# Where the operands of a matmul start: new addresses for the rows of x and for the weight slots

## The chip, the cores and the metric

The kernel runs on one core of one Trainium2 chip. The metric is the time of one execution on the device, in microseconds (us).

## The reference

One layer of a hybrid encoder on 512 tokens of 2048 features, with 16 learned meta tokens ahead of them (528 rows). What matters here is where its matrix products are:

```
hn = rmsnorm(h_res, norm_in_g)
P = hn @ w_in                       # 528 x 2048 times 2048 x 8320
Pr, Pc = P[..., :4224], P[..., 4224:]
...                                 # Pr: r, k, v, gate, two low-rank inputs -> RWKV-7 state recurrence
...                                 # Pc: B, C, h, gate -> gated causal convolution of width 3
h_res = h_res + concat(y_a, y_b) @ w_out
return rmsnorm(h_res, norm_f_g)[16:]
```

All of it is in float32. The kernel keeps that precision with products in the round format float32r: each operand is split into a high part and a low part (the remainder), and a product is made of three matmuls: high by high, high by low, low by high.

## The kernel before

**Input projection.** `x`, transposed and multiplied by the norm's gain, lies in SBUF as two tiles of 16 rows of 528 numbers, `xh` (high) and `xl` (low); row `kt` holds features 128 kt to 128 kt + 127 of all 528 tokens, one feature a partition. `w_in` is cut into 65 tiles of 128 output columns. The list `plan` gives their order: the low-rank tile, then k, r, B, v and so on, for eight pairs of heads (k, r, v, g) and eight groups of the convolution (C, h, B, gc). A weight tile comes in as two transfers of 128 x 1024 numbers (`raw`, three buffers), and each half of a transfer, a quarter of the tile, is split into `hi` and `lo` of 128 x 512 (`split_w`, lines 121 to 126: the copy on ACT at line 124, the subtraction on DVE or POOL at line 125). There are six buffers for `hi` and six for `lo`; a quarter is split about six quarters before its use (`prefetch`).

`steps` (lines 305 to 317) issues the matmuls: for a quarter, each range of columns, each of four `kt`, and the three products

```
for n, (ww, xx) in enumerate(((hi, xh), (hi, xl), (lo, xh))):
    nc.tensor.matmul(ps[r], ww[:, w], xx[:, kt, a:b], ...)
```

Here `ww[:, w]`, 128 x 128, is the operand that is loaded into the array (the trace has each load as an instruction of PEld), and `xx[:, kt, a:b]` is the one that streams past it. The ranges are FULL (k, v and the low-rank tile: columns 0 to 264 and 264 to 528), TAIL (r, g, C, h: 14 to 272 and 272 to 528) and REAL (B, gc: 16 to 528 in one). A tile of two ranges has 96 matmuls, one of REAL has 48; line 314 has 5,466 matmuls in all.

**Order of the work.** TensorE's program is written by hand: `mains` is a generator that yields after each main matmul, and the other stages (low-rank products, Gram matrices, the inversion and the recurrence over chunks) call `fill` to put so many main matmuls between their own. So while weights remain, PE has work beside nearly every wait.

**Output projection.** `units` lists 56 products of 128 x 1024 weights with sums and differences of the mixed activations (a Strassen-like scheme with seven products instead of eight). Here the operands change places: the activations (`parts`, tiles m0 and m1, and `sform`, tiles S1, S3, S4, S5) are loaded into the array, and the split weights, again `hi` and `lo`, stream with 512 columns (`product`, line 1220). Their splits are made by ACT (line 1192) and DVE (line 1193) in the same six buffers, `oh` and `ol`. Only the last product's weights have buffers of their own, the `home` tiles, laid over the S tiles of the first half; they stream at line 1220 with 512 columns and at line 1422 with 256.

**Where tiles lie.** A pool hands out memory in the order in which its tiles are asked for, each rounded up to 32 bytes; the pools `cp`, `wp`, `xp`, `tp` stand one behind the other from the low end of a partition, `keep` and `cq` from the high end; `pw` takes the place of `xp` and `tp` once they are closed, `ch` and `pp` the place of `cq`. Before the change `xh`, `xl`, every `hi` and every `lo` start at one residue modulo 512 bytes. A row of `xh` is 528 x 4 = 2112 bytes, 64 more than a multiple of 512. The S tiles and m tiles start 160 bytes further modulo 512 than the streaming `oh` and `ol`, and `home` tiles start at the same residue as the m tiles beside them.

Of the kernel before, what the change touches and what calls it, by code (L numbers as in the profile page):

```python
# [9 lines left out]
F32 = mybir.dt.float32  # L10
F32R = mybir.dt.float32r
I32 = mybir.dt.int32
# [6 lines left out]
P = 128  # L19
DM = 2048  # L20
KT = DM // P
SEQ = 512
META = 16
L = SEQ + META
CH = 64
NCH = SEQ // CH + 1
# [6 lines left out]
C_ID, C_GM, C_BM, C_HS, C_ON = 0, 128, 384, 512, 514  # L33
C_N = 515
# [12 lines left out]


AHEAD, WEIGHTS = 6000, 3000


def _constants():
# [24 lines left out]
def hymba_kernel(ctx: ExitStack, tc: tile.TileContext, xt, xtok, front, w_in, w_out, pv, lup, cst, msk, gf, out):  # L77
    nc = tc.nc
    ctx.enter_context(tc.manual_schedule(engines={mybir.EngineType.PE}))
    cp = ctx.enter_context(tc.tile_pool(name="cp", bufs=1))  # L80
    dp = ctx.enter_context(tc.tile_pool(name="dp", bufs=2, space=DRAM))
    wp = ctx.enter_context(tc.tile_pool(name="wp", bufs=3))

    pvt = cp.tile([P, V_N], F32, name="pvt")
    cs = cp.tile([P, C_N], F32, name="cs")
    ms = cp.tile([P, CH], I32, name="ms")
    mhalf = cp.tile([P, 8], F32, name="mhalf")
    nc.gpsimd.memset(mhalf, -0.5)
    ident = cs[:, C_ID : C_ID + P]
    gmask = cs[:, C_GM : C_GM + 256].rearrange("p (h c) -> p h c", h=2)  # L90
    opd = [dp.tile([NCH * P * OPW], F32, tag=f"opd{j}", name=f"opd{j}", bufs=1) for j in range(NPAIR)]
    rbd = [dp.tile([P, SEQ], F32, tag=f"rbd{j}", name=f"rbd{j}", bufs=1) for j in range(NPAIR)]
    gated = [dp.tile([P, SEQ], F32, tag=f"gated{j}", name=f"gated{j}", bufs=1) for j in range(NPAIR)]
# [11 lines left out]
    plan = [("lora", 0), ("k", 0), ("r", 0), ("B", 0), ("v", 0), ("k", 1), ("r", 1), ("v", 1), ("g", 0), ("g", 1)]  # L105
# [8 lines left out]
        stream += [w_in[m, :, 0:1024], w_in[m, :, 1024:2048]]  # L114
    stream[0:8] = [stream[j] for j in (0, 2, 4, 6, 1, 3, 5, 7)]
    N_IN = len(stream)
    stream += [w_out[0, g] for g in range(3)]
    quarters, chain, low = {}, {}, {}
    state = {"next": 0}

    def split_w(q, rq, eng):
        hi = wp.tile([P, 512], F32R, tag="hi", name=f"wh{q}", bufs=6)
        lo = wp.tile([P, 512], F32R, tag="lo", name=f"wl{q}", bufs=6)
        nc.scalar.copy(hi, rq)  # L124
        low[q] = eng.tensor_tensor(out=lo, in0=rq, in1=hi.bitcast(F32), op=ALU.subtract).ins  # L125
        quarters[q] = (hi, lo)
# [13 lines left out]
    cq = ph2.enter_context(tc.tile_pool(name="cq", bufs=1, side="right", reuse_waits="tile"))  # L140
    ph1 = ExitStack()
    xp = ph1.enter_context(tc.tile_pool(name="xp", bufs=1))
    xh = xp.tile([P, KT, L], F32R, name="xh")
    xl = xp.tile([P, KT, L], F32R, name="xl")
    rs = xp.tile([P, L], F32, name="rs")
    la = xp.tile([P, 2, L], F32R, name="la")
    ones = xp.tile([P, P + 2], F32R, name="ones")
    omm = xp.tile([P, 33], F32, name="omm")
    hv = xp.tile([P, 6, 8], F32, name="hv")
    hl = cp.tile([P, 2, 8], F32, name="hl")  # L150
    smask = xp.tile([P, NCH, CH], F32, name="smask")
    pm = ph1.enter_context(tc.tile_pool(name="pm", bufs=4, space=PSUM))
    pz = ph1.enter_context(tc.tile_pool(name="pz", bufs=2, space=PSUM))
    pi = ph1.enter_context(tc.tile_pool(name="pi", bufs=1, space=PSUM))
# [8 lines left out]
    def tm(name):  # L163
        return tp.tile([P, LP], F32, tag="tm", name=name, bufs=3)
# [50 lines left out]


    for n in range(4):
        quarters[2 * n] = tuple(
            wp.tile([P, 512], F32R, tag=tag, name=f"w{tag[0]}{2 * n}", bufs=6) for tag in ("hi", "lo")
        )  # L220
    F0, F1, F2 = KT + P + L, 4 * P + L, 8 * P + 2 * L
    fr = [view("bt", F0), view("r0", 3 * P), view("bk", F1), view("gt0", F2)]
    o = 0
# [74 lines left out]
        )  # L298

    nc.scalar.copy(ones, cs[:, C_BM : C_BM + P + 2])  # L300
    FULL = ((0, 264), (264, L))
    TAIL = ((14, 272), (272, L))
    REAL = ((META, L),)

    def steps(ps, ranges, k4, q, ks=range(4), rs_=range(2)):
# [25 lines left out]
    def scaled(ranges, ps, dst, base):  # L331
        for (a, b), p in zip(ranges, ps):
            nc.vector.tensor_tensor(out=dst[:, a - base : b - base], in0=p, in1=rs[:, a:b], op=ALU.mult)

    def shift_full(ps, m, name, dst):
        pr = tp.tile([P, L + 1], F32, tag="pr", name=f"pr_{name}", bufs=2)
        nc.gpsimd.memset(pr[:, 0:1], 0.0)
        scaled(FULL, ps, pr, -1)
        sh = tm(f"sh_{name}")[:, 0:L]
        nc.scalar.activation(sh, pr[:, 0:L], AF.Copy, scale=col(V_MU, m))  # L340
        for (a, b), d in dst:
            nc.vector.scalar_tensor_tensor(
                out=d, in0=pr[:, a + 1 : b + 1], scalar=omm[:, m : m + 1], in1=sh[:, a:b], op0=ALU.mult, op1=ALU.add
            )

    def shift_real(ps, m, name, dst):
        pr = tp.tile([P, L + 1], F32, tag="pr", name=f"pr_{name}", bufs=2)
        scaled(TAIL, ps, pr, 14)
        sh = tm(f"sh_{name}")[:, 0:SEQ]
        nc.scalar.activation(sh, pr[:, 1 : SEQ + 1], AF.Copy, scale=col(V_MU, m))  # L350
        nc.vector.scalar_tensor_tensor(
            out=dst, in0=pr[:, 2 : SEQ + 2], scalar=omm[:, m : m + 1], in1=sh, op0=ALU.mult, op1=ALU.add
        )
# [25 lines left out]
    def use(what, i, ps):  # L379
        if what == "lora":  # L380
            use_lora(ps)
        elif what in ("k", "v"):
            t = cq.tile([P, LP], F32, tag=what, name=f"{what}{i}")
            nc.gpsimd.memset(t[:, META:CH], 0.0)
            shift_full(ps, tile_of[what] + i, f"{what}{i}", padded(t))
            got[what, i] = t
        elif what in ("r", "g"):
            t = cq.tile([P, SEQ], F32, tag=f"r{i % 2}" if what == "r" else "g", name=f"{what}{i}")
            shift_real(ps, tile_of[what] + i, f"{what}{i}", t)
            if what == "g":  # L390
                gate(t, f"r{i}")
                later(14000, lambda: nc.sync.dma_start(gated[i], t))
            got[what, i] = t
        elif what == "C":
            u = tm(f"u{i}")
            scaled(TAIL, ps, u, 14)
            got[what, i] = u
        elif what == "h":
            u = got["C", i]
            hh = tm(f"hh{i}")  # L400
            with behind_of("turned"):
                scaled(TAIL, ps, hh, 14)
            n = SEQ + 2
            nc.gpsimd.tensor_tensor(out=u[:, 0:n], in0=u[:, 0:n], in1=hh[:, 0:n], op=ALU.mult)
            cv = tp.tile([P, SEQ], F32, tag="cw", name=f"cv{i}")
            nc.scalar.activation(cv, u[:, 0:SEQ], AF.Copy, scale=col(V_CW, i))
            for j in (1, 2):
                nc.vector.scalar_tensor_tensor(
                    out=cv, in0=u[:, j : j + SEQ], scalar=col(V_CW, 8 * j + i), in1=cv, op0=ALU.mult, op1=ALU.add
                )  # L410
            got[what, i] = cv
            if i == 0:
                nc.gpsimd.tensor_tensor(out=cv, in0=cv, in1=got["B", 0], op=ALU.mult)
        elif what == "B":
            b = tm(f"b{i}")[:, 0:SEQ] if i else tp.tile([P, SEQ], F32, name="b0")
            with behind_of("split"):
                scaled(REAL, ps, b, META)
            got[what, i] = b
            if i:
                nc.gpsimd.tensor_tensor(out=got["h", i], in0=got["h", i], in1=b, op=ALU.mult)  # L420
        else:
            cv = got["h", i]
            g = tm(f"gc{i}")[:, 0:SEQ]
            scaled(REAL, ps, g, META)
            gate(g, f"c{i}")
            o = direct.get(8 + i, cv)
            nc.vector.scalar_tensor_tensor(out=o, in0=cv, scalar=0.5, in1=g, op0=ALU.mult, op1=ALU.mult)
            if o is cv:
                later(9000, lambda: nc.sync.dma_start(mixd[8 + i], cv))
        ready.add((what, i))  # L430
# [29 lines left out]
    def mains():  # L460
# [34 lines left out]
        use("B", 0, pd)  # L495
        for j in range(4, len(plan)):
            what, i = plan[j]
            rg = FULL if what in ("k", "v") else REAL if what in ("B", "gc") else TAIL
            ps = yield from main(j, rg, f"{what}{i}")
            if what == "B" and i < 4:  # L500
                state["split"] = low[4 * j + 4]
            use(what, i, ps)
# [620 lines left out]

    pw = ctx.enter_context(tc.tile_pool(name="pw", bufs=1, reuse_waits="tile"))
    po = ctx.enter_context(tc.tile_pool(name="po", bufs=8, space=PSUM, reuse_waits="tile"))
    ssq = pw.tile([P, 4, 5], F32, name="ssq")
    fv = pw.tile([P, 4, 3], F32, name="fv")
    sform = {
        (f, q): [pw.tile([P, 4, HT], F32R, tag=f"{f}{q}{a}", name=f"{f}{q}{a}") for a in range(2)]
# [54 lines left out]
    def split_unit(unit, t, home=None):  # L1184
        for q in range(2):
            rq = t()[:, q * 512 : (q + 1) * 512]
            if home is None:
                hi = wp.tile([P, 512], F32R, tag="hi", name=f"oh{U[unit]}{q}", bufs=6)
                lo = wp.tile([P, 512], F32R, tag="lo", name=f"ol{U[unit]}{q}", bufs=6)
            else:  # L1190
                hi, lo = home[q]
            nc.scalar.copy(hi, rq)
            nc.vector.tensor_tensor(out=lo, in0=rq, in1=hi.bitcast(F32), op=ALU.subtract)  # L1193
            right[unit, q] = (hi, lo)
# [301 lines left out]
```

## Time and profile before

| | before |
|---|---|
| time, median of 3 runs (lowest to highest) | 1025.84 us (1023.99 to 1026.12) |
| span of the profiled execution, first to last instruction | 1023.6 us |
| PE busy | 1006.6 us (98%), 9,723 matmuls |
| DVE busy | 686.1 us (67%) |
| ACT busy | 393.8 us (38%) |
| POOL busy | 273.8 us (27%) |

The profiled execution has no time of its own beside the span; the median of the runs is 2.2 us longer than the span. In the profile PE is the matrix engine with its matmuls, PEld its loads of the stationary operand, DVE the vector engine, ACT the scalar engine, POOL the general one, SP the engine that issues most transfers. A line of a group reads: source line, engine, operation, output tile <- input tiles, shapes, count | busy time in us, mean duration in ns | idle time of the engine just ahead of it and what ended it. In the timeline and in the chain of waits the first number is the start in us from the span's begin and the second the length; `xN` counts the instructions that the line holds. A row of windows holds, behind the stretch and its length, the busy time and count of PE, PEld, DVE, ACT and POOL, then the granted clock, the share of the DMA engines and GB/s.

### The profile page before, as it was taken

Reading aid. Unit: us, or ns where it says so; the run is one execution under the profiler, and the core shown is the slowest. Engines: PE = TensorE matmul, PEld = TensorE weight load, DVE = VectorE, ACT = ScalarE, POOL = GpSimd, SP = SyncE. Lnnn points to the kernel's source line nnn. Section 1 sums busy time; section 2 is a strip of 40 time slices with the busy share of each in tenths; the row PEclk is TensorE's granted clock in tenths of the full one; section 3 lists DMA queues with packets and bytes.
Section 4 is the critical chain, followed back from the end, with each engine's and each line's share of the span. In section 5 each row is a group of like instructions: output and inputs, shape, how many; then the busy total and the mean of one; then the engine's idle time right before and its main releaser. Section 6 shows DMA issues by size and latency. Waiting matters only on the chain.

```text
span 1023.6 us, 23708 instructions
## 1 busy us (share of the span) xinstructions
PE 1006.6 (98%) x9723; PEld 919.0 (90%) x9723; DVE 686.1 (67%) x1239; ACT 393.8 (38%) x729; POOL 273.8 (27%) x292
## 2 busy tenths in 40 slices
PE   9999999999999999999999999999999999999996
PEld 8899998999988999998999998889889897787885
DVE  7677954587765569654669653244555697998787
ACT  7553423344313434322434322222222335445453
POOL 0122323233332323232322232123332332015001
PEclk9999999999999999999999999999999999999999
DMA  9526476546764364864263845867673688695754
GB/s 333 152 63 148 122 190 182 150 123 143 167 172 134 96 170 99 217 167 117 83 166 98 220 139 168 309 212 235 195 232 93 183 276 192 172 319 135 172 125 165
DMA packets 185036, 174.82 MB, mean 171 GB/s; under 512 B 121568, under 2 KB 142816, under 8 KB 184416
## 3 DMA queue, kind: packets, MB, share of 16 engines
q1 hardware_dynamic: 182336, 164.40, 55.8%
q0 software_dynamic: 2304, 8.39, 4.7%
q8 instruction: 76, 1.25, 0.5%
q10 hardware_dynamic: 288, 0.52, 0.1%
q14 instruction: 32, 0.26, 0.1%
HBM read 136.92 MB, written 36.35 MB: 169 GB/s over the span
## 4 chain that ended last, share of the span: by engine, by line
PE 68%; DVE 8%; DMA 4%; issue 2%; SPq 1%; ACT 1%; POOL 0%; DVEq 0%; ACTq 0%; POOLq 0%
PE ps_gc L314 8%; PE ps_h L314 8%; PE ps_B L314 7%; PE ps_k L314 7%; PE ps_v L314 7%; PE ps_C L314 7%; PE ps_g L314 7%; PE ps_r L314 7%; DVE ol L1193 3%; DMA wo<-in_w_out_dram 2%; PE M L1220 2%; PE g L659 1%; PE zs L984 1%; PE Q L1220 1%; DVE xb L1201 1%
## 5 line engine op out<-in xcount | busy, mean ns | idle before, releaser
L125 POOL TENSOR_TENSOR wl<-wr,wh 128x512 fp32r<-128x512 f32 x119 | 169.2, 1423 | 370.8 <-ACT wh L124 356.4
L124 ACT CAST wh<-wr 128x512 fp32r<-128x512 f32 x252 | 152.7, 618 | 294.8 <-PE ps_C L314 51.9
L125 DVE TENSOR_TENSOR wl<-wr,wh 128x512 fp32r<-128x512 f32 x133 | 100.9, 765 | 109.0 <-ACT wh L124 108.6
L314 PE MATMUL ps_k<-xh,wl 128*128 128x264 f32 x256 | 73.1, 286 | 1.1 <-DVE wl L125 1.1
L314 PE MATMUL ps_v<-xh,wh 128*128 128x264 f32 x256 | 73.0, 285 | 0.0
L314 PE MATMUL ps_h<-xh,wh 128*128 128x258 f32 (+1 forms) x256 | 72.8, 284 | 0.0
L314 PE MATMUL ps_k<-xh,wh 128*128 128x264 f32 x256 | 72.8, 284 | 0.0
L314 PE MATMUL ps_v<-xl,wh 128*128 128x264 f32 x256 | 72.7, 284 | 0.0
L314 PE MATMUL ps_v<-xh,wl 128*128 128x264 f32 x256 | 72.7, 284 | 0.0
L314 PE MATMUL ps_k<-xl,wh 128*128 128x264 f32 x256 | 72.6, 284 | 0.0
L314 PE MATMUL ps_C<-xh,wh 128*128 128x258 f32 (+1 forms) x256 | 72.6, 284 | 0.0
L314 PE MATMUL ps_h<-xh,wl 128*128 128x258 f32 (+1 forms) x256 | 72.3, 282 | 0.2 <-issue 0.2
L314 PE MATMUL ps_r<-xh,wh 128*128 128x258 f32 (+1 forms) x256 | 72.4, 283 | 0.0
L314 PE MATMUL ps_g<-xl,wh 128*128 128x258 f32 (+1 forms) x256 | 72.3, 282 | 0.0
L314 PE MATMUL ps_r<-xl,wh 128*128 128x258 f32 (+1 forms) x256 | 72.2, 282 | 0.0
L314 PE MATMUL ps_g<-xh,wl 128*128 128x258 f32 (+1 forms) x256 | 72.0, 281 | 0.0
L314 PE MATMUL ps_C<-xl,wh 128*128 128x258 f32 (+1 forms) x256 | 72.0, 281 | 0.0
L314 PE MATMUL ps_g<-xh,wh 128*128 128x258 f32 (+1 forms) x256 | 72.0, 281 | 0.0
L314 PE MATMUL ps_h<-xl,wh 128*128 128x258 f32 (+1 forms) x256 | 71.9, 281 | 0.0
L314 PE MATMUL ps_r<-xh,wl 128*128 128x258 f32 (+1 forms) x256 | 71.9, 281 | 0.0
L314 PE MATMUL ps_C<-xh,wl 128*128 128x258 f32 (+1 forms) x256 | 71.9, 281 | 0.0
L314 PE MATMUL ps_B<-xh,wl 128*128 128x512 f32 x128 | 51.3, 401 | 0.0
(353 smaller groups left out, 3006.2 us busy)
## 6 DMA issues: line engine op xcount, KB each, us to landing
wr<-in_w_in_dram SPq DMA_DIRECT2D x126, 512.0 KB
ct<-opd SPq DMA_DIRECT2D x64, 288.0 KB
wo<-in_w_out_dram SPq DMA_DIRECT2D x24, 512.0 KB
x<-in_w_out_dram POOLq DMA_DIRECT2D x16, 512.0 KB, 6.2
opd<-ar SPq DMA_DIRECT2D x8, 576.0 KB
opd<-gt SPq DMA_DIRECT2D x16, 288.0 KB
opd<-bt SPq DMA_DIRECT2D x64, 64.0 KB
x<-in_w_out_dram SPq DMA_DIRECT2D x8, 512.0 KB
```

The lines of the kernel that those rows point to most:

```text
L124: nc.scalar.copy(hi, rq)
L125: low[q] = eng.tensor_tensor(out=lo, in0=rq, in1=hi.bitcast(F32), op=ALU.subtract).ins
L314: nc.tensor.matmul(ps[r], ww[:, w], xx[:, kt, a:b], start=(kt == 0 and n == 0), stop=(kt == KT - 1 and n == 2))
L659: nc.tensor.matmul(z[h][:, c - c0], bk[hs, c, h : h + 2, :].rearrange("p a s -> p (a s)"), ar[hs, c].rearrange("p a s -> p (a s)"), start= ...
L984: nc.tensor.matmul(d[hs, j], w, x[hs], start=(a == 0), stop=(a == b - 1))
L1193: nc.vector.tensor_tensor(out=lo, in0=rq, in1=hi.bitcast(F32), op=ALU.subtract)
L1201: nc.vector.tensor_tensor(out=h, in0=h, in1=ps, op=op)
L1220: nc.tensor.matmul(bank[s], left(prod, jj, m, s), w, start=(jj == 0 and n == 0), stop=(jj == 7 and n == 2))
```

## The change

The change gives new addresses to the operands of the main and the output products. It adds and removes no instruction of the computation.

- `xh` and `xl` become parts of one tile `xx` with 16 rows of 1152 numbers (9 x 512 bytes): the high part at 0, the low part at 528.
- `hi` and `lo` of a quarter become parts of one slot of 1152 numbers; six slots. In the main stage the high part starts at `column(j)` numbers, a number that depends on the weight tile, and the low part 528 behind it. So each of the three matmuls of a product, at every `kt`, has the same distance modulo 512 bytes between the operand that is loaded and the one that streams, for a whole weight tile. `column` is 8 i for k, r, C and B and 8 i + 56 for v, g, h and gc, with i from 0 to 7: fifteen values from 0 to 112.
- FULL becomes 0 to 256 and 256 to 528, TAIL 14 to 270 and 270 to 528. C and h keep the old TAIL under the name WIDE.
- In the output stage `hi` starts at 112 and `lo` at 624 of a slot, and `ssq` takes 92 numbers instead of 20, which moves the S tiles behind it. Streaming and loaded operands then start at one residue modulo 512 bytes.
- The constants `cs` and `ms`, the tiles `la`, `ones`, `omm`, `hv`, `smask` and the buffers `pr` and `b0` move from `cp`, `xp` and `tp` to `cq`.

```diff
+SLOT, XROW, XL_AT, OUT_AT = 1152, 1152, L, 112
...
+    def column(j):
+        what, i = plan[j]
+        return {
+            "k": 8 * i, "v": 8 * i + 56, "r": 8 * i, "g": 8 * i + 56, "C": 8 * i, "h": 8 * i + 56, "B": 8 * i, "gc": 8 * i + 56, "lora": 0,
+        }[what]
...
+    def slot(name, at, gap):
+        t = wp.tile([P, SLOT], F32R, tag="w", name=name, bufs=6)
+        return t[:, at : at + 512], t[:, at + 512 + gap : at + 1024 + gap]
+
+    def slot_of(q):
+        if q >= 2 * N_IN:
+            return slot(f"w{q}", OUT_AT, 0)
+        n = q // 2
+        return slot(f"w{q}", column(n % 4 if n < 8 else n // 2), XL_AT % 128)
+
     def split_w(q, rq, eng):
-        hi = wp.tile([P, 512], F32R, tag="hi", name=f"wh{q}", bufs=6)
-        lo = wp.tile([P, 512], F32R, tag="lo", name=f"wl{q}", bufs=6)
+        hi, lo = slot_of(q)
...
-    xh = xp.tile([P, KT, L], F32R, name="xh")
-    xl = xp.tile([P, KT, L], F32R, name="xl")
+    xx = xp.tile([P, KT, XROW], F32R, name="xx")
+    xh, xl = xx[:, :, 0:L], xx[:, :, XL_AT : XL_AT + L]
...
-    FULL = ((0, 264), (264, L))
-    TAIL = ((14, 272), (272, L))
+    FULL = ((0, 256), (256, L))
+    TAIL = ((14, 270), (270, L))
+    WIDE = ((14, 272), (272, L))
...
-            rg = FULL if what in ("k", "v") else REAL if what in ("B", "gc") else TAIL
+            rg = FULL if what in ("k", "v") else REAL if what in ("B", "gc") else WIDE if what in ("C", "h") else TAIL
...
-    ssq = pw.tile([P, 4, 5], F32, name="ssq")
+    ssq = pw.tile([P, 92], F32, name="ssq")[:, 0:20].rearrange("p (a b) -> p a b", b=5)
...
-                hi = wp.tile([P, 512], F32R, tag="hi", name=f"oh{U[unit]}{q}", bufs=6)
-                lo = wp.tile([P, 512], F32R, tag="lo", name=f"ol{U[unit]}{q}", bufs=6)
+                hi, lo = slot(f"o{U[unit]}_{q}", OUT_AT, 0)
```

More of the change, by code (lines that the diff above doesn't have):

```diff
@@ L84, in hymba_kernel @@
     pvt = cp.tile([P, V_N], F32, name="pvt")
-    cs = cp.tile([P, C_N], F32, name="cs")
-    ms = cp.tile([P, CH], I32, name="ms")
     mhalf = cp.tile([P, 8], F32, name="mhalf")
     nc.gpsimd.memset(mhalf, -0.5)
-    ident = cs[:, C_ID : C_ID + P]
-    gmask = cs[:, C_GM : C_GM + 256].rearrange("p (h c) -> p h c", h=2)
     opd = [dp.tile([NCH * P * OPW], F32, tag=f"opd{j}", name=f"opd{j}", bufs=1) for j in range(NPAIR)]
@@ L142, in hymba_kernel @@
     xp = ph1.enter_context(tc.tile_pool(name="xp", bufs=1))
-    xh = xp.tile([P, KT, L], F32R, name="xh")
-    xl = xp.tile([P, KT, L], F32R, name="xl")
+    xx = xp.tile([P, KT, XROW], F32R, name="xx")
+    xh, xl = xx[:, :, 0:L], xx[:, :, XL_AT : XL_AT + L]
     rs = xp.tile([P, L], F32, name="rs")
[L146 to L149, printed above, removed]
+    la = cq.tile([P, 2, L], F32R, name="la")
+    ones = cq.tile([P, P + 2], F32R, name="ones")
+    omm = cq.tile([P, 33], F32, name="omm")
+    hv = cq.tile([P, 6, 8], F32, name="hv")
     hl = cp.tile([P, 2, 8], F32, name="hl")
-    smask = xp.tile([P, NCH, CH], F32, name="smask")
+    smask = cq.tile([P, NCH, CH], F32, name="smask")
+    cs = cq.tile([P, C_N], F32, name="cs")
+    ms = cq.tile([P, CH], I32, name="ms")
+    ident = cs[:, C_ID : C_ID + P]
+    gmask = cs[:, C_GM : C_GM + 256].rearrange("p (h c) -> p h c", h=2)
     pm = ph1.enter_context(tc.tile_pool(name="pm", bufs=4, space=PSUM))
@@ L217, in hymba_kernel @@
     for n in range(4):
-        quarters[2 * n] = tuple(
-            wp.tile([P, 512], F32R, tag=tag, name=f"w{tag[0]}{2 * n}", bufs=6) for tag in ("hi", "lo")
-        )
+        quarters[2 * n] = slot_of(2 * n)
     F0, F1, F2 = KT + P + L, 4 * P + L, 8 * P + 2 * L
@@ L335, in shift_full @@
     def shift_full(ps, m, name, dst):
-        pr = tp.tile([P, L + 1], F32, tag="pr", name=f"pr_{name}", bufs=2)
+        pr = cq.tile([P, L + 1], F32, tag="pr", name=f"pr_{name}", bufs=2)
         nc.gpsimd.memset(pr[:, 0:1], 0.0)
@@ L346, in shift_real @@
     def shift_real(ps, m, name, dst):
-        pr = tp.tile([P, L + 1], F32, tag="pr", name=f"pr_{name}", bufs=2)
+        pr = cq.tile([P, L + 1], F32, tag="pr", name=f"pr_{name}", bufs=2)
         scaled(TAIL, ps, pr, 14)
@@ L395, in use @@
             u = tm(f"u{i}")
-            scaled(TAIL, ps, u, 14)
+            scaled(WIDE, ps, u, 14)
             got[what, i] = u
@@ L401, in use @@
             with behind_of("turned"):
-                scaled(TAIL, ps, hh, 14)
+                scaled(WIDE, ps, hh, 14)
             n = SEQ + 2
@@ L414, in use @@
         elif what == "B":
-            b = tm(f"b{i}")[:, 0:SEQ] if i else tp.tile([P, SEQ], F32, name="b0")
+            b = tm(f"b{i}")[:, 0:SEQ] if i else cq.tile([P, SEQ], F32, name="b0")
             with behind_of("split"):
```

## The prediction

> **What bounds the kernel now.** I read the page first, then the chain of work that ended last in order of time, then the windows of the output stage, then start times in the timeline. The page:
>
> ```profile
> span 1023.6 us, 23708 instructions
> PE 1006.6 (98%) x9723; PEld 919.0 (90%) x9723; DVE 686.1 (67%) x1239; ACT 393.8 (38%) x729; POOL 273.8 (27%) x292
> PEclk9999999999999999999999999999999999999999
> ```
>
> PE is busy for 98% of the span at the full granted clock, so the pace of the matmul stream sets the time. A matmul's own duration says little of that pace (several are in the pipe at once); the distance between starts says it. The chain gives it for whole weight tiles:
>
> ```profile
> 328.81 11.65 PE ps_k L314 x96
> ...
> 430.32 11.36 PE ps_C L314 x96
> ...
> 844.06 11.14 PE ps_gc L314 x48
> ```
>
> The first has 96 matmuls of 264 columns in 11.65 us, 121.4 ns each. The second has 96 of 258 or 256 columns in 11.36 us, 118.3 ns each. The third has 48 of 512 columns in 11.14 us, 232.1 ns each. From the second to the third that is 113.8 ns for 255 columns, 0.446 ns a column and 3.6 ns a matmul. Now the same pace where the weight load beside the stream is only two columns wide:
>
> ```profile
> 224.92 0.29 PE L691 MATMUL n<-sq_h,ones 128*2 128x288 f32 x1
> 225.05 0.30 PE L692 MATMUL n<-sq_l,ones 128*2 128x288 f32 x1
> 225.18 0.30 PE L691 MATMUL g<-sq_h,ones 128*2 128x288 f32 x1
> 225.31 0.30 PE L692 MATMUL g<-sq_l,ones 128*2 128x288 f32 x1
> ```
>
> Three spacings in 0.39 us are 130 ns for 288 columns; the line above gives 3.6 + 288 x 0.446 = 132 ns. So a full load beside the stream costs, on average over the addresses that this kernel uses, about nothing. The change moves only addresses, so what it can give is a shift between good and bad addresses.
>
> **Is there such a shift?** The two output loops show it, both with 512 columns:
>
> ```profile
> 870.08 0.39 PE L1220 MATMUL M<-ol,S 128*128 128x512 f32 x1
> ...
> 872.18 0.39 PE L1220 MATMUL M<-ol,S 128*128 128x512 f32 x1
> ...
> 1004.76 4.71 PE L1220 MATMUL end<-home,m 128*128 128x512 f32 x20
> 1009.31 5.91 PE L1422 MATMUL end<-home,m 128*128 128x256 f32 x48
> L1220 PE MATMUL end<-home,m 128*128 128x512 f32 x24 | 5.6, 390 | 0.0
> ```
>
> From 870.08 to 872.18 lie nine matmuls: 233.3 ns each. The home group has 20 in 4.71 us; less the last one's 390 ns that is 4.32/19 = 227.4 ns. Same columns, same loop; what differs is the tile that streams. By the tile sizes (each rounded to 32 bytes), the weights of an ordinary unit start 160 bytes (40 elements) before the left operand modulo 512, the home tiles at the same residue as it. I call the second operand's start minus the streaming one's, modulo 128 elements, the distance. In the main loop all pools between are multiples of 512 bytes, so it is -(16 kt + a), with a the first column of the range: every tile walks through eight distances now.
>
> ```profile
> L314 PE MATMUL ps_k<-xh,wl 128*128 128x264 f32 x256 | 73.1, 286 | 1.1 <-DVE wl L125 1.1
> L314 PE MATMUL ps_v<-xl,wh 128*128 128x264 f32 x256 | 72.7, 284 | 0.0
> ...
> L314 PE MATMUL ps_gc<-xl,wh 128*128 128x512 f32 x128 | 50.9, 398 | 0.0
> L314 PE MATMUL ps_r<-xl,wh 128*128 128x258 f32 x128 | 36.3, 283 | 0.0
> L314 PE MATMUL ps_r<-xl,wh 128*128 128x256 f32 x128 | 35.9, 280 | 0.0
> ```
>
> From the start times of the matmuls in the first two and the four like groups (1,577 spacings, 87 to 102 at each distance), the mean at 264 columns is 120.4 ns at distance 0 and 119.8 at 64, 122.7 at 24, 122.4 at 32 and 122.2 at 40. Multiples of 16 average 121.1, odd multiples of 8 average 122.0. The curve is real but only 3 ns high. In the same way the groups like the last three give 230.8 ns for gc and B at distance 0 (79 spacings), and for r, g, C and h 119.5 ns at 258 columns and 117.6 at 256.
>
> **The change part by part.**
>
> *k and v tiles.* Each gets one distance, 0 to 56 for k and 56 to 112 for v, the same eight residues that both ranges sweep now. Mean of the curve at the new sixteen: 121.5 ns, against 121.6. I take 0. Splitting 528 columns 256 + 272 for 264 + 264 moves no column: 0.
>
> *r and g.* The second range begins at 270 for 272. Before, its distances are multiples of 16 and its 256 columns take 117.6 ns; the first range, 2 off such a multiple, takes 119.5 ns for 258 (means above). Two columns explain 0.9 of the 1.9 ns; 1.0 is the price of the odd start. The change makes both ranges odd: 16 tiles x 48 matmuls x 1.0 ns = +0.8 us.
>
> *C and h.* The second range keeps 272, with half the tiles at odd multiples of 8: 768 x 0.5 x 1.0 ns = +0.4 us.
>
> *B and gc.* All 768 matmuls sit on multiples of 16 now, half would not: 768 x 0.5 at 1.0 to 2.0 ns (512 columns pass twice as many addresses) = +0.4 to +0.8, taken +0.6 us.
>
> Main stage together +1.8 us. No row shows a tile held at one distance throughout, so its unknown is bounded by the ends of the curve, 119.8 and 122.7 around the mean 121.6: for 5,466 matmuls -9.8 to +6.0 us. I stay at the mean, since fifteen distances spread over the whole curve.
>
> *Output.* With OUT_AT = 112 and the larger ssq all 624 matmuls that are not home come to distance 0. At 233.3 - 227.4 = 5.9 ns that is 3.7 us at most. But the stage has a second bound:
>
> ```profile
> 855.00:930.00 75.00, 73.90 (x314) 58.45 (x313) 72.04 (x94) 42.32 (x72) 11.56 (x10) 1.00 0.77 215
> 930.00:1003.60 73.60, 73.13 (x311) 57.88 (x310) 59.17 (x85) 35.36 (x65) 12.26 (x12) 1.00 0.59 137
>   DVE ol L1193: 6.0, 12
> ```
>
> The columns after the length are PE, PEld, DVE, ACT and POOL. In the first half DVE is busy 72.04 of 75 us (96%), and PE already waits for its splits 12 times, 6.0 us (by the releasers). A PE 2.5% faster meets that wait again, so half of 314 x 5.9 = 1.9 us stays: 0.9. In the second half DVE has 14 us to spare: 311 x 5.9 = 1.8 us. Output -2.7 us; the lower bound, from the main loop's gc and B at distance 0 (230.8 ns), is 624 x 2.5 ns x about 0.75 = -1.2 us.
>
> *One slot for both halves.* The copy on ACT into a slot now waits for the matmul that reads the low half too, one later than the high half's last, 0.23 us at most. Behind it on ACT queue only evacuations and the next copies. PE wants that slot six quarters later, and a quarter lasts 24 x 121 ns = 2.9 us, while the copy and split on POOL take about 0.6 + 1.3 us:
>
> ```profile
> L124 ACT CAST wh<-wr 128x512 fp32r<-128x512 f32 x252 | 152.7, 618 | 294.8 <-PE ps_C L314 51.9
> L125 POOL TENSOR_TENSOR wl<-wr,wh x119: 1269/1292/3001, 62.0 to 843.3; 128x512 fp32r<-128x512 f32 x119
> ```
>
> Cost 0; without the cover it would be 252 x 0.23 us, which ten microseconds of lead exclude.
>
> *Tiles moved to the right-hand pool.* They carry no new instruction and no DMA; the scan's chunk tiles now lie on the masks and constants, whose last readers come before the last inverse is stored, which those loads follow on SP's queue anyway. 0.
>
> **Sum:** +1.8 - 2.7 = -0.9 us, span 1022.7. The runs' median 1025.84 is 2.2 us above this execution's span; I add it: 1024.9 us. A measurement of this kernel tells 0.2% (2.05 us) from no change.
>
> **A rule against the change.** The Trainium skill, page "TensorE: Matmul & The Clock Gate", Part 2, step 1, has two independent SBUF read ports, so that loading the next weights takes no read bandwidth from the running matmul. By it neither distance nor slot matters and the time stays 1025.8. The average (130 against 132 ns) agrees; the pair 227.4 against 233.3 ns does not.
>
> **The rivals.**
>
> 1. *Faster: constant distance sharpens the curve.* Home matmuls, all at distance 0, run at 227.4 ns; gc and B meet distance 0 only in passing and take 230.8 there. If tiles held at one distance in its good half gain like that, 3.4 ns at 512 columns and half of it for the short ones, half the tiles give 0.5 x (768 x 3.4 + 4,698 x 1.7) = 5.3 us, and with the output 2.7: 1018 us. Against it: the 256-column row.
>
> 2. *Slower: the short matmul has no room beside its load.* The home group of 256 columns, also at distance 0, takes (5.91 - 0.283)/47 = 119.7 ns (0.283 is its duration, row below), against 117.6 for 256 columns in the walking loop: +2.1 ns. Its load reads for most of that time:
>
> ```profile
> L1422 PE MATMUL end<-home,m 128*128 128x256 f32 x48 | 5.9, 283 | 0.0
> L1422 PEld LDWEIGHTS end<-home,m 128*128 128x128 f32 x48 | 5.9, 192 | 0.1
> L988 PEld LDWEIGHTS zy<-st,ct 64*64 64x64 f32 x224 | 11.1, 134 | 0.0
> ```
>
> 64 more columns lengthen a load by 58 ns, so 128 read for about 116 of 119.7 ns. If every short matmul of the main stage, at one fixed distance, pays this, 4,698 x 2.1 = +9.9 us, less 2.7: 1033 us. It decides from 0.6 ns a short matmul, where it has eaten the output's gain. For it: 48 of one kind with one pace. Against it: the curve's own low end lies at distance 0.
>
> 3. *Addresses do nothing* and 233.3 against 227.4 is a difference of the products: 1025.8 us.
>
> **Chances.** Forecast 0.42 (1022 to 1028; of it 0.13 below the 0.2% line, 0.27 within, 0.02 above), rival 1 0.25 (faster), rival 2 0.25 (slower), rival 3 0.08 (within). So faster 0.38, within 0.2% 0.35, slower 0.27; the forecast's own range is 1022 to 1028. To leave out no more than 2 in 10 the range goes from just below rival 1 to rival 2: 1016 to 1033.
>
> **What would show it.** The chain's whole tiles: k, r, C and B of low index against high should differ by up to 3 ns a matmul, with the mean of k and v staying at 121.5 ns; r and g 0.5 ns longer. Output nines at 227 to 228 ns for 233.3, home unchanged, and more PE idle behind DVE's ol than 6.0 us before 930. Wrong if all short tiles move one way (rivals 1 and 2), if output stays at 233, or if PE waits for wh or wl in the main loop.

## The result, and the profile after

The changed kernel takes 1028.58 us (median of 7 runs, 1027.31 to 1029.63) against 1024.19 us (7 runs, 1023.18 to 1026.12) of the kernel before on the same chip: ratio 1.0039, 95% interval [1.0027, 1.0050]. It is slower. In three later sets the kernel before had medians of 1025.39 (25 runs), 1025.45 (29) and 1025.95 us (12), so the loss is nearer 3 than 4 us. Each ratio below is to the kernel before in the same set. The profiled executions have spans of 1023.6 and 1026.3 us, 2.7 us apart. After the change the line numbers move: the main matmuls stand at line 329, the output's at 1234, the splits at 136 and 137 in the main stage and 1206 and 1207 in the output; `hi` and `lo` are both called `w` or `o`.

The head of the page, after:

```profile
span 1026.3 us, 23687 instructions
...
PE 1007.3 (98%) x9723; PEld 921.8 (90%) x9723; DVE 685.4 (67%) x1239; ACT 393.3 (38%) x729; POOL 276.9 (27%) x292
```

The busy times hardly moved. As in the prediction, the pace is read from whole tiles in the chain of waits (start, length, count):

```profile
330.25 11.77 PE ps_k L329 x96
...
394.30 11.77 PE ps_v L329 x96
418.74 14.08 PE ps_g L329 x117
432.82 11.40 PE ps_C L329 x96
482.13 11.57 PE ps_k L329 x96
...
545.85 11.56 PE ps_v L329 x96
570.14 14.11 PE ps_g L329 x117
584.25 11.44 PE ps_C L329 x96
...
802.09 11.19 PE ps_gc L329 x48
```

Here the distance is that between the streaming operand and the one that is loaded beside it, for the next matmul: in the timeline of before, the matmul `M<-ol` and the load of `M<-oh` behind it both start at 870.08 us. This distance is the same for all three matmuls of a product; between a matmul's own two operands it is not, since the low part of the weights lies 16 numbers further modulo 128 than the high part.

Tiles of one kind now differ, as they should if the distance matters: k at distance 32 takes 122.6 ns a matmul and at 48 takes 120.5; v at 96 takes 122.6 and at 112 takes 120.4 (before, such a tile took 11.65 or 11.66 us, 121.4 ns, whichever it was). But the dear ones outweigh the cheap ones, and both g rows are dearer than the same rows of before, which are

```profile
416.49 13.83 PE ps_g L314 x117
...
567.32 13.83 PE ps_g L314 x117
```

In the output, the timeline of PE after:

```profile
892.15 2.88 PE L1234 MATMUL Q<-o,S 128*128 128x512 f32 x12
894.87 2.88 PE L1234 MATMUL P<-o,S 128*128 128x512 f32 x12
897.59 2.65 PE L1234 MATMUL M<-o,S 128*128 128x512 f32 x11
```

Twelve matmuls from 892.15 to 894.87 are 226.7 ns each, against 233.3 before. So the output's pace rose as forecast. What PE waited for at that line, after:

```profile
its engine sat idle before it (us, times) until:
  DVE o L1207: 8.9, 17
  ACT o L1206: 2.3, 3
```

It was 6.0 us, 12 times, for DVE (and 0.2 us, once, for ACT) before. The waits ate most of the gain.

From the start times of all matmuls (spacings under 140 ns, or 245 ns for 512 columns, give the pace; what longer ones exceed 233 ns by gives the waits of the output, which come out smaller than by the releasers):

| | before | after | effect, us |
|---|---|---|---|
| k, v, ns a matmul | 121.5, 121.6 | 121.9, 122.1 | +0.7 |
| r, g | 118.7, 118.6 | 120.1, 120.0 | +2.1 |
| C, h | 118.5, 118.5 | 119.1, 119.0 | +0.8 |
| B, gc | 231.9, 231.9 | 232.1, 232.2 | +0.2 |
| output, without home | 233.4 | 227.3 | -3.8 |
| waits in the output, us | 3.2 | 6.1 | +2.9 |
| sum | | | +2.9 |

### The profile page after: what moved, and what is told of

Read it like the earlier page. It is cut to its first block, busy times and chain, and to the rows that moved or that the text cites. A ratio compares the mean times of both kernels' runs of the same rounds, so it can differ in the third digit from the quotient of the medians.

```text
span 1026.3 us, 23687 instructions
## 1 busy us (share of the span) xinstructions
PE 1007.3 (98%) x9723; PEld 921.8 (90%) x9723; DVE 685.4 (67%) x1239; ACT 393.3 (38%) x729; POOL 276.9 (27%) x292
## 4 chain that ended last, share of the span: by engine, by line
PE 60%; DVE 6%; issue 2%; DMA 1%; ACT 1%; POOL 0%; DVEq 0%; ACTq 0%; POOLq 0%
PE ps_gc L329 8%; PE ps_B L329 7%; PE ps_h L329 7%; PE ps_C L329 7%; PE ps_v L329 5%; PE ps_k L329 5%; PE ps_g L329 5%; PE ps_r L329 5%; PE M L1234 4%; DVE o L1207 2%; PE P L1234 1%; PE Q L1234 1%; PE zs L999 1%; PE zy L1003 1%; DMA wo<-in_w_out_dram 1%
## 5 line engine op out<-in xcount | busy, mean ns | idle before, releaser
L136 ACT CAST w<-wr 128x512 fp32r<-128x512 f32 x252 | 153.1, 618 | 305.7 <-PE ps_k L329 47.6
L137 POOL TENSOR_TENSOR w<-wr,w 128x512 fp32r<-128x512 f32 x119 | 168.0, 1413 | 371.4 <-ACT w L136 310.8
L137 DVE TENSOR_TENSOR w<-wr,w 128x512 fp32r<-128x512 f32 x133 | 97.5, 739 | 112.1 <-ACT w L136 101.1
L329 PE MATMUL ps_r<-xx,w 128*128 128x256 f32 (+1 forms) x768 | 98.8, 283 | 0.0
L329 PE MATMUL ps_k<-xx,w 128*128 128x256 f32 (+1 forms) x768 | 97.4, 285 | 1.1 <-DVE w L137 1.1
L329 PE MATMUL ps_v<-xx,w 128*128 128x256 f32 (+1 forms) x768 | 97.7, 285 | 0.0
L329 PEld LDWEIGHTS ps_k<-xx,w 128*128 128x128 f32 x768 | 95.2, 188 | 2.1 <-DVE w L137 1.4
L329 PE MATMUL ps_B<-xx,w 128*128 128x512 f32 x384 | 96.1, 401 | 0.0
L329 PE MATMUL ps_h<-xx,w 128*128 128x258 f32 (+1 forms) x768 | 95.8, 283 | 0.3 <-issue 0.3
L329 PEld LDWEIGHTS ps_v<-xx,w 128*128 128x128 f32 x768 | 95.2, 188 | 0.3
```

Source lines behind the costliest of these rows:

```text
L329: nc.tensor.matmul(ps[r], ww[:, w], xx[:, kt, a:b], start=(kt == 0 and n == 0), stop=(kt == KT - 1 and n == 2))
```

## The experiments

The theory after this reading had three parts: **(1)** r and g pay for where their streaming operand starts; **(2)** the output's gain is real, but the splits ahead of it come late; **(3)** one distance through a tile gives a sharp price curve, of which the fifteen distances use all, dear and cheap. The rival to the second was that DVE simply has too much to do in the output.

**The output back at distance 40** (e1):

```diff
-SLOT, XROW, XL_AT, OUT_AT = 1152, 1152, L, 112
+SLOT, XROW, XL_AT, OUT_AT = 1152, 1152, L, 72
```

> The changed kernel with the output slots at 72 instead of 112: the output products are back at a distance of 40 elements, the main stage keeps its new addresses. Theory (the main stage costs +3.2 us; in the output the faster stream of 227.3 ns gives 3.8 us, of which DVE's splits take 2.9 back): output spacing back at 233.4 ns, PE's waits for DVE's o back from 8.9 to about 6 us, time +0.7 to +1.5 us against the changed kernel, main stage unchanged at 3.2 us over the kernel before. Rival (the new layout, one slot for both halves, slows the output stage by itself and the distance does not matter): spacing stays near 227 ns or waits stay near 9 us, time as the changed kernel or 3.8 us above it.

Measured: 1028.48 us (6 runs), ratio to before 1.0037 [1.0022, 1.0051]. Two rows of its timeline:

```profile
891.34 2.96 PE L1234 MATMUL Q<-o,S 128*128 128x512 f32 x12
894.14 2.96 PE L1234 MATMUL P<-o,S 128*128 128x512 f32 x12
```

2.80 us for twelve, 233.3 ns: the distance alone makes and unmakes the 6.6 ns. Waits in the output are 4.1 us for 6.1, so 2.0 of 3.8 us come back, and e1 should take 1.8 us more than the changed kernel. Yet the time cannot be told from it, where 0.7 to 1.5 us more were expected. The two profiles hide such a loss: near 309 us the changed kernel has a stretch of slower matmuls that costs 1.3 us (last section), and e1 has none. The runs do not show the loss either, but their intervals, about 1.5 us either way, leave room for most of it. The 4.1 us are also more than the 3.2 us of before: 1.7 us of them stand at product 3 (the 56 products have twelve matmuls each and are numbered from 0), where before had 0.1 us. Something else in the change adds a wait there.

**r and g, two edits.** e2 gives r and g their old ranges, 14 to 272 and 272 to 528; e3 leaves the ranges and shifts the weights instead, so that the distance is a multiple of 8 while the streaming operand still starts at column 14 or 270:

```diff
-            rg = FULL if what in ("k", "v") else REAL if what in ("B", "gc") else WIDE if what in ("C", "h") else TAIL
+            rg = FULL if what in ("k", "v") else REAL if what in ("B", "gc") else WIDE
... (TAIL becomes WIDE at the other places of r and g too)
```

```diff
-            "k": 8 * i, "v": 8 * i + 56, "r": 8 * i, "g": 8 * i + 56, ...
+            "k": 8 * i, "v": 8 * i + 56, "r": 8 * i + 6, "g": 8 * i + 54, ...
```

> The changed kernel with the ranges of r and g back at 14 to 272 and 272 to 528; all else as changed. Theory (a range that starts at column 270 lies 2 elements off a multiple of 8 and pays for it): the second range of r and g goes from about 120.0 to 118.5 ns at 256 columns, both ranges from a mean of 120.05 to about 119.0, which is 1,536 x 1.0 ns = -1.6 us against the changed kernel. Rival (r and g are slower by their columns' distances alone, wherever the range starts): mean stays at 120.0 ns and the time within 0.3 us of the changed kernel.

> The changed kernel with the slots of r and g moved by +6 (r) and -2 (g) elements: the ranges still start at columns 14 and 270, but the distance of r and g is now a multiple of 8 in both ranges, while the slots themselves start 6 elements off a multiple of 8. If the distance decides: r and g fall from 120.05 to about 119.0 ns, -1.6 us against the changed kernel. Rival (the start of the streaming operand decides, columns 14 and 270 being 8 bytes off a multiple of 16 bytes): they stay at 120.0 ns. A third outcome, above 120.5 ns, would mean that the loaded operand's own start has a price too.

Measured: e2 1026.15 us (10 runs), 1.0009 [1.0000, 1.0017]; e3 1028.28 us (10 runs), 1.0027 [1.0018, 1.0036]. The g rows in the chain of e2 and then of e3:

```profile
415.86 13.99 PE ps_g L329 x117
...
567.02 13.82 PE ps_g L329 x117
```

```profile
417.12 13.94 PE ps_g L329 x117
...
568.24 14.17 PE ps_g L329 x117
```

The two rows add up to 28.19 us in the changed kernel, 27.81 in e2 and 28.11 in e3. Over all r and g matmuls the mean falls from 120.0 to 119.0 ns in e2 and stays at 119.9 in e3. So the new ranges cost 1.0 ns a matmul, 1.6 us in all, and a distance made a multiple of 8 does not take it away. The theory of the odd distance found no support, and what the rival given with e3 forecast came true. It is not shown, though, that the start of the streaming operand, 8 bytes off a multiple of 16 bytes at columns 14 and 270, is the cause. e3 puts the loaded operand 8 bytes off too, and a price of that could stand in for the other. And by range, the mean spacings do not fit a price of the start alone:

| r and g | first range | second range |
|---|---|---|
| before | 258 columns from 14: 119.5 ns | 256 from 272: 117.7 ns |
| after | 256 from 14: 119.9 | 258 from 270: 120.1 |
| e2 | 258 from 14: 119.6 | 256 from 272: 118.4 |
| e3 | 256 from 14: 119.8 | 258 from 270: 120.0 |

From e2 to after the second range takes 1.8 ns more, of which its two more columns explain 0.9. The first starts at 14 in both and takes 0.3 ns more with two columns fewer, 1.2 ns at equal columns; what changes there is its end, 270 for 272. No run separates start, end and length.

**The best distances** (e4): what the changed kernel's own tiles show of the curve, used for all tiles.

```diff
-            "k": 8 * i, "v": 8 * i + 56, "r": 8 * i, "g": 8 * i + 56, "C": 8 * i, "h": 8 * i + 56, "B": 8 * i, "gc": 8 * i + 56, "lora": 0,
+            "k": 112, "v": 112, "r": 72, "g": 72, "C": 72, "h": 72, "B": 0, "gc": 0, "lora": 112,
```

with r and g on WIDE as in e2.

> The changed kernel with one column for each kind of tile, the cheapest that the changed kernel's own tiles show, and r and g on the ranges 14 to 272 and 272 to 528: k, v and the low-rank tile at 112, B and gc at 0 (distance 112), r, g, C and h at 72 (distances 58 and 56). Theory (each distance has its price, whatever the tile): 256 + 272 columns 240.9 ns a pair for 244.0, 258 + 256 columns 235.9 for 240.1 (r, g) and 238.1 (C, h), 512 columns 230.2 for 232.15; 768 of each: -2.4 -3.2 -1.7 -1.5 = -8.8 us against the changed kernel, about 1019.8 us, below the kernel before by some 4.4 us. Rival (the differences between the changed kernel's tiles come from what runs beside them, or a distance kept by all tiles wears out): spacings stay at the means, 122.0, 119.5 and 232.1 ns, and the time at 1027 to 1029 us.

Measured: 1021.65 us (6 runs), 0.9964 [0.9952, 0.9976], faster than both kernels. The whole tiles of k, v, g, C and gc in its chain are now all as cheap as the cheapest of their kind in the changed kernel, or cheaper:

```profile
327.60 11.56 PE ps_k L329 x96
...
414.67 13.80 PE ps_g L329 x117
428.47 11.32 PE ps_C L329 x96
...
795.44 11.08 PE ps_gc L329 x48
```

The pace gave 7.4 us of the 8.8 expected; k and v came to 120.6 and 120.8 ns, r, g, C, h to 117.8 to 118.1, but B and gc to 231.6 and 231.2 and not to 230.2. The third part of the theory holds for k, v, r, g, C and h. B and gc have another price beside the distance: at the one distance 112 their tiles take 230.5 to 232.5 ns. e4 also shows that a start 8 bytes off has no fixed price. The first ranges of r, g, C and h still start at column 14, and at distance 58 their 258 columns take 117.8 to 118.1 ns, no more than the 256 columns from 272 beside them (117.9 to 118.0).

**The output alone** (e5), on the kernel before, with the main stage untouched:

```diff
-    ssq = pw.tile([P, 4, 5], F32, name="ssq")
+    ssq = pw.tile([P, 108], F32, name="ssq")[:, 0:20].rearrange("p (a b) -> p a b", b=5)
     fv = pw.tile([P, 4, 3], F32, name="fv")
+    pad = pp.tile([P, 40], F32, name="pad")
```

> The kernel before, main stage untouched; only the output operands get distance 0 (ssq takes 108 numbers, a pad of 160 bytes follows the m tiles). The new chain tile x03 stays over tiles that are free early. Theory A (the output gain is real, and a late transfer of x03 ate part of it in the changed kernel): spacing of the output matmuls 233.4 to 227.4 ns, 3.8 us; DVE's splits give about 1.5 us of it back; x03 is still requested about 7 us ahead of the output's start; time 2.0 to 2.8 us under before (ratio about 0.9977). Rival B (the split engine DVE is the bound of the output stage and gives back nearly all, whatever x03 does): ratio 0.9990 to 1.0. Rival C (nothing is given back): 3.8 us, 0.9963.

Measured: 1024.55 us (12 runs), 0.9987 [0.9976, 0.9998]. The pace went from 233.4 to 227.2 ns (-3.85 us), the waits from 3.2 to 5.6 us (+2.4); 1.4 us are left, and the runs gain 1.3 us. That is a gain between the two forecasts, nearer to the rival's: 2.4 us come back where 1.5 were expected. e1 moves the streaming operand and e5 the loaded one, and the same two paces come out: it is the distance between the two that counts, not the place of either.

**The late transfer.** Beside the waits that e5 has, the changed kernel has a longer one at product 3: 1.6 us with the two spacings behind it, 0.99 us of them at once, for 0.4 us in e5 and 0.1 us before. The trace leads to it: the weights `x03` of product 3 are requested by SP and split by ACT. Before, in the timeline of SP and ACT (start, length) and in the waits of SP (total, times, longest, us):

```profile
847.46 0.33 SPq L1169 DMA_DIRECT2D x<-in_w_out_dram  x1
...
861.52 2.17 ACT L1192 CAST oh<-x 128x512 fp32r<-128x512 f32 x4
```

```profile
SPq L1169 <- POOL cv L420: 1.3, 1, 1.3
```

and after:

```profile
861.37 0.33 SPq L1184 DMA_DIRECT2D x<-in_w_out_dram  x1
...
866.78 2.18 ACT L1206 CAST o<-x 128x512 fp32r<-128x512 f32 x4 [1.93 <-DMA x<-in_w_out_dram]
```

```profile
SPq L1184 <- DVE mix L442: 11.9, 1, 11.9
```

The output begins at 855.0 and at 858.3 us. The request, 7.6 us ahead of it before, now comes 3.1 us behind it, because it waits for DVE's last mixing product (line 442). In SBUF `x03` lay over a buffer shared by tiles such as `b` and `gc` and over a buffer `pr`, read long before; with `pr` moved to `cq` everything behind it slid down, and `x03` came to lie over `cv`, which that product reads. Two edits test this. e6 asks for the two `sh` tiles ahead of `x03` in the changed kernel, so that `x03` lies where no tile was:

```diff
     xa = [pw.tile([P, 1024], F32, name=f"xa{t}") for t in range(4)]
+    early = [pw.tile([P, 512], F32, tag=f"sh{s}", name=f"sh0{s}") for s in range(2)]
... (the first row half uses them in place of its own)
```

e8 does the reverse to the kernel before: the same two tiles and one tile of the tag `sqj` ahead of `x03` put it over `cv`. e7 is e4 with e6's edit.

> The changed kernel with the two sh tiles asked for ahead of x03, so that x03 lies on 4096 bytes that no tile of the main stage holds. Theory A: its transfer is issued some 13 us earlier, ACT no longer waits 1.9 us for x<-in_w_out, the 1.0 us wait of PE at the third M1 product goes, and the first half of the output loses 1.0 to 1.9 us; time about 1.2 us under the changed kernel, 1027.3, ratio to before about 1.002. Rival B (DVE bounds the stage anyway): the wait moves to the next splits, time as the changed kernel's, 1.0035.

> The version with the best distances of the main stage (columns 112, 72 and 0, ranges from 14 to 272) with the same move of x03. Theory A: 1.2 us under that version's 1021.65, so about 1020.4, ratio to before 0.9952. Rival B: 0.9964 as before the move.

> The kernel before with x03 put over the tiles cv that the last mixing product reads, as in the changed kernel, and nothing else moved: the late transfer alone. Theory A: the request of x03 moves from about 7 us ahead of the output's start to about 3 us behind it; PE waits about 1.0 us more at the third M1 product; time 0.8 to 1.5 us above before, ratio 1.0008 to 1.0015. Rival B: no difference, since the splits behind it bound the stage.

Measured: e6 1027.87 us (12 runs), 1.0021 [1.0011, 1.0031]; e7 1020.16 us (6 runs), 0.9944 [0.9931, 0.9957]; e8 1027.38 us (12 runs), 1.0016 [1.0006, 1.0026]. In e8, with nothing else changed, the request and the wait are as in the changed kernel:

```profile
857.98 0.33 SPq L1171 DMA_DIRECT2D x<-in_w_out_dram  x1
...
863.25 2.18 ACT L1194 CAST oh<-x 128x512 fp32r<-128x512 f32 x4 [1.80 <-DMA x<-in_w_out_dram]
```

In e6 and e7 the request stands at 850.56 and 844.00 us, ACT does not wait for it, and the wait at product 3 is down to 0.3 and 0.4 us; the waits of the output fall by 1.1 us from the changed kernel to e6 and by 1.8 us from e4 to e7. In e8's profile the wait at product 3 rises from 0.1 to 1.2 us, but later ones shrink, so that all together rise by 0.6 us only, less than its runs lose (1.6 us, at least 0.6). All three point one way; the size is 0.6 to 1.8 us.

**Amount or order of the splits.** What is left of the waits could be DVE's load, which moving work about would not lessen, or the order of its queue. In the second half of e7's output ACT stands in front of the `home` splits:

```profile
979.40 1.14 ACT L1207 CAST home<-wo 128x512 fp32r<-128x512 f32 x2 [5.00 <-DMA wo<-in_w_out_dram]
980.45 1.14 ACT L1207 CAST o<-wo 128x512 fp32r<-128x512 f32 x2
```

The `o` split behind it is wanted first: PE waits at product 46 for it, and reads no `home` tile before product 52. From e7, e9 asks for the splits of `home` two products later, e10 makes the sums and S tiles of the second row half two products later, e11 does both:

```diff
-        split_unit(
-            (1, "M2", g), passing(1, 1, 0, g),
+        at(
+            28 + 15 + 2 * g, split_unit, (1, "M2", g), passing(1, 1, 0, g),
```

```diff
         if n == 2:
-            at(n + 1, sums, 1)
-        at(6 + n, split_form, f, 1)
+            at(5, sums, 1)
+        at(8 + n, split_form, f, 1)
```

> The version with the best distances and x03 moved, and one thing more: the splits of the four home tiles are asked for two products later (their transfers at the same place). Theory A (the late waits of PE, units 45 to 50, come from the order of ACT's queue: it stands 7.8 us at home <- DMA wo, with the splits of the next products behind it): those waits, about 1.3 us, go, the others stay; time about 1.2 us under 1020.2, so 1019.0. Rival B (DVE's amount of work bounds the stage): the waits come back at other products, time 1020.2.

> The same base, and instead of the home splits the sums and S tiles of the second row half are made two products later (sums at product 5 for 3, S tiles at 8 to 11 for 6 to 9). Theory A (order, not amount): the waits of PE at products 6, 7 and 9, about 2.1 us with their tails, fall under 0.7 us; time about 1.4 us under 1020.2, so 1018.8. Rival B (DVE has 96% to do in the first half of the output, so what is put off is late somewhere else): waits of the same sum appear at products 10 to 16, time 1020.2.

> Both of these together on the same base. Theory A: 2.6 us under 1020.2, so about 1017.6, ratio to before 0.9925; waits of the output stage 4.9 to about 2 us. Rival B: 1020.2, 0.9944.

Measured: e9 1018.55 us (5 runs), 0.9928 [0.9914, 0.9942]; e10 1018.40 us (6 runs), 0.9930 [0.9915, 0.9945]; e11 1017.80 us (5 runs), 0.9917 [0.9902, 0.9932]. The waits at the output line, e7 and then e11:

```profile
its engine sat idle before it (us, times) until:
  DVE o L1208: 8.6, 16
  ACT o L1207: 0.2, 1
```

```profile
its engine sat idle before it (us, times) until:
  DVE xa L1216: 1.3, 2
  ACT S L1154: 1.2, 1
  DVE o L1208: 1.0, 3
```

The waits in spacings fall from 4.9 us in e7 to 3.7 in e9, 3.1 in e10 and 1.9 in e11. In e9 those behind product 45 are gone and no others came; in e10 those at products 6, 7 and 9 fell from 2.2 to 1.3 us, not under the 0.7 expected, and none came at 10 to 16. It was mostly the order: DVE's busy time is 686.5 us in e7 and 685.5 in e11, while 3.0 us of 4.9 are gone. What is left waits for `xa`, S and `o` tiles by the rows above, and was not tried further. The gaps between the ratios of e9, e10 and e7 are about as large as the intervals, so for these the trace decides more than the time.

**k and v with equal ranges** (e12): `FULL` back to 0 to 264 and 264 to 528 in the changed kernel.

> The changed kernel with FULL back at 0 to 264 and 264 to 528, so k and v keep the one distance of each tile but have two ranges of 264 columns. Theory A (256 and 272 columns are dearer together than twice 264, since 272 has its own price curve): k and v come back to 121.5 ns from 122.0, 0.7 us less, 1027.9. Rival B (one distance through a whole tile costs it): they stay at 122.0.

Measured: k 121.7 and v 121.6 ns (from 121.9 and 122.1), so 0.5 of the 0.7 us were the split into 256 and 272. The time, 1029.03 us (7 runs), 1.0035 [1.0022, 1.0047], does not show so small a thing. Why unequal ranges cost more than equal ones was not tried further.

## Why the prediction was wrong, point by point

**What bounds the kernel: right.** The pace of PE's stream sets the time, addresses move it, and a few nanoseconds on thousands of matmuls are microseconds.

**r and g: the mechanism was wrong and so was the size.** The text priced "the odd start" at 1.0 ns by distance, for the second range, and put the first at nothing; both rose, by 1.4 ns on the mean: +2.1 for +0.8 us. By e2 the new ranges cost 1.6 us of it, and by e3 a distance that is a multiple of 8 does not mend that. The other 0.5 us stay with the old ranges, as in C and h. The rows at 258 columns could not tell distance from start, since there both were off together; which property of the ranges costs the 1.6 us stays open.

**k and v, C and h: sizes.** Taken at the mean of the old curve, 0 and +0.4; measured +0.7 and +0.8. Splitting into 256 and 272, put at 0 because it "moves no column", costs 0.5 us by e12. In C and h the second range rose by 0.6 ns, 0.5 us, about as forecast; the first, put at nothing, rose by 0.4 ns, 0.3 us, though its columns did not change. So the curve at a held distance is not the curve in passing. At 256 columns odd multiples of 8 do cost 1.0 ns more on the mean, the price that was used, but not one by one: 117.4 to 118.0 ns at 112, 48, 0, 64 and 16, and 119.1 to 119.9 at 24 to 40, 88 and 104, while 56, an odd multiple, takes 118.1. B and gc came out better, +0.2 for +0.6. The main stage together: +3.8 for +1.8 us.

**Output pace: right.** 226.7 to 227.4 ns for 227 to 228 forecast, and 3.8 us for 3.7.

**Output waits: the step that failed most.** The text let the first half lose half its gain and the second half keep all, because DVE "has 14 us to spare" there: 1.0 us lost. 2.9 us were. An idle share is no slack: in e5, with `x03` early, the first half gave back 0.6 us and the second 1.8 (its waits from product 45 on went from 0.2 to 1.9 us), although DVE had those 14 us to spare: ACT stood at `home <- DMA wo` for 9.4 us in three waits (7.8 before) with the next splits queued behind. In e9 these waits went by order alone. In the changed kernel, with `x03` late, the halves gave back 1.8 and 1.1 us.

**Tiles moved: 0 was wrong.** The text looked at the tiles that were moved and not at what lies on their old place. That moved `x03`, whose transfer became late; 0.6 to 1.8 us by e6, e7 and e8.

**Merged slot: right.** No new wait of PE for `w` in the main stage is seen.

**The rivals.** The first (a held distance sharpens the curve) was right in its mechanism and wrong in its sum: the fifteen distances hold dear and cheap ones alike. e4, which takes only cheap ones, shows what was in it. The second is not what happened: with e4's distances the short matmul of the main stage is faster than before, not slower, so there is room beside its load. Why the 48 home matmuls of 256 columns stay at 119.9 ns in every run, at the distance at which the main stage's take 117.6, is open. The third is ruled out by the pair of the changed kernel and e1: 226.7 against 233.3 ns by an offset of 160 bytes between the loaded and the streaming operand, with the same instructions. The rule that the prediction took from the Trainium skill, page "TensorE: Matmul & The Clock Gate", Part 2, step 1, that loading the next weights takes no read bandwidth from the running matmul, does not fit this pair if it is read to mean that the distance does not matter. Whether the two operands have read ports of their own no run here shows, nor what they collide in.

So the sum of -0.9 became +2.9 us: 2.0 in the main stage and 1.9 in the output's waits, less 0.1 of pace.

## What to carry to other kernels

Where PE is the bound, measure the price of each distance between the loaded and the streaming operand, for the very ranges of columns in use, before spreading tiles over many: choose the cheap ones, since a spread only averages. Moving the bounds of a range is a change of its own: two columns more or less cost about 1 ns a matmul here beside what the columns themselves take. When a tile is moved or resized, list what now overlies what, for a transfer into it waits for the last reader of whatever lay there. A faster stream does not help where in-order queues ahead of it hold a needed split behind one that is needed later; look at the order of the queue before its load.

## What the runs showed of the hardware

The price by distance, in the changed kernel, for tiles held at one distance: 117.4 ns (112) to 119.9 (88) at 256 columns, 123.5 (112) to 126.3 (72) at 272, 230.1 (112) to 233.8 (80) at 512 columns; at every one of these widths 112 is the cheapest, and 48 lies within 0.4 ns of it. Each figure at 256 columns is a mean of one to three tiles, and tiles at one distance can differ: 120.9 and 118.7 ns at 88, 119.2 and 116.7 at 96. So the distance is not the whole of the price.

A stretch of half clock comes and goes. In the profile of before, PE waits 2.24 us for DVE, and the first spacings of 512 columns behind the wait, from 307.52 us on, are 591, 427, 427, 426 and 405 ns, where 232 is usual. In e2's the wait is 2.06 us and nothing follows. The timeline and the windows (clock third from last) there, first of before, then of e2:

```profile
306.45 1.14 PE L831 MATMUL t<-xn,gt 64*64 64x64 f32 x32 [2.24 <-DVE xn L822]
```

```profile
308.00:312.00 4.00, 4.00 (x18) 2.86 (x17) 0.69 (x1) 2.11 (x5) 1.29 (x1) 0.78 0.60 204
```

```profile
307.06 0.69 PE L846 MATMUL t<-xn,gt 64*64 64x64 f32 x32 [2.06 <-DVE xn L837]
```

```profile
307.00:311.00 4.00, 3.94 (x46) 3.10 (x46) 0.70 (x2) 2.35 (x5) 0.96 (x1) 1.00 0.66 223
```

The granted clock is 0.78 in one and 1.00 in the other; over the five slow spacings alone, 307.52 to 309.80 us, it is 0.51. The stretch costs 1.1 us in before (2,276 ns for five spacings of 232) and 1.3 us after, so it makes only 0.2 us of their difference. Over 66 runs of the kernel before, those with a mean clock of 0.998 took 1024.4 us (15) and those with 0.996 1026.2 (34), but 7 runs with 0.995 took 1025.1, so the clock is not the whole of the spread. What decides whether the stretch comes stays open.
